# Moving operands at the top of each SBUF partition, weights at the bottom, and four block layouts in the four SwiGLUs

## The chip, the cores and the metric

The kernel runs on one core of one Trainium2 chip. The metric is the time of one execution on the device in microseconds (us). The core has a matrix engine (TensorE, written PE in the profile, with its weight loads listed apart as PEld), a vector engine (DVE), a scalar engine (ACT), a general engine (POOL) and a queue engine (SP). SBUF is the on-chip memory that the engines read. It has 128 partitions, and an address in this text is a byte offset within a partition. PSUM is the memory into which TensorE writes its products.

## What is computed

The reference is a trunk of four residual layers on 256 tokens of 1024 features. Each layer has a token mixer and then a SwiGLU, each behind an RMS norm:

```python
for i in range(DEPTH):                       # DEPTH = 4
    h = rmsnorm(x, norm_mix_g[i])
    # i % 3 == 0: short gated convolution; 1: neighbourhood attention; 2: Hyena long convolution
    x = x + mixer(h)
    x = x + swiglu(rmsnorm(x, norm_ffn_g[i]), f_w13[i], f_w2[i])

def swiglu(h, w13, w2):                      # w13: 1024 x 5632, w2: 2816 x 1024
    g, u = jnp.split(h @ w13, 2, axis=-1)
    return (jax.nn.silu(g) * u) @ w2
```

Layers 0 and 3 use the convolution (mixer A), layer 1 the attention (mixer B), layer 2 the Hyena mixer (mixer C). The Hyena filters depend on the weights alone.

## The kernel before

**Layout.** Features lie on the partitions and the 256 tokens along them, so that every weight is the stationary operand of a matmul (what a weight load, LDWEIGHTS, puts into the array, 128 x 128) and the activations stream past it (the moving operand, 128 x 256).

**Products in three parts.** Every float32 operand is split into a high and a low part of the type float32r. `wload` (line 98) brings a weight piece of 128 x 1024 into a staging tile `st` by a DMA on SP's queue, copies it to `hi` on ACT (line 105) and subtracts to get `lo` on DVE or POOL (the helper on line 74). `mm3` (line 113) then issues three matmuls for each 128 x 128 block: hi by the high part of the moving operand (line 116), hi by its low part (line 117), lo by its high part (line 118). Each has a weight load of its own.

**A SwiGLU** (`ffn`, line 259) first makes 44 column tiles of the gate and up products into the accumulators `pg` and `pu`: 8 blocks, 3 matmuls each, with the normed input `xs` moving (8 tiles `xsf`, each with the high and the low part side by side). That is 1056 matmuls in a layer. `gated` makes the hidden activation and splits it (`split`, line 122) into 11 tiles `hid`. Then come 8 output tiles `po` (line 300) of 22 blocks, taken from weight pieces of 8, 7 and 7 blocks: 528 matmuls with `hid` moving. The mixers use the same helpers, with `xsm` moving in their input products and `mid` tiles in their output products. In mixer B's input product the weights move and `xsm` is the stationary operand.

**Where the tiles lie.** All pools are allocated upwards from one end: constants and `X` first, then `xsp` (`xs`), `wst` (`st`), `wsp` (`hi` and `lo`), the scratch pools, and behind them what a stage needs (`hid`, `mid`, tables). Counting the sizes of the tiles in that order, with the 16 KB and some small constants that the runtime and the compiler keep at the bottom, `xs` begins at 26.0 KB, `hi` at 62.0 KB, `lo` at 86.0 KB. `xs`, `hi` and `lo` tiles are 2 or 4 KB long, so their starts differ by whole multiples of 1 KB. The stage tiles do not keep that: the start of `hid` modulo 1 KB is 672 bytes in layers 0 and 1 and 128 bytes in layers 2 and 3; that of `mid` is 128 bytes in mixers A and C and 800 bytes in mixer B.

**What sets the order.** The source issues everything in the order of use; a scheduler then orders each engine's queue by dependences, among them the reuse of an address by a later tile. The Hyena filters' tables (`filters`, line 542: `dec`, 1 MB, and `dfth`, 512 KB, loaded on ACT's and POOL's queues) share addresses with the `mid` tiles of the first mixer A, and so wait for its output product. The filters' products (`ff`, line 606) are woven into the first two SwiGLUs.

Of the kernel before, what the change touches and what calls it, by code (L numbers as in the profile page):

```python
# [18 lines left out]
P = 128  # L19
# [10 lines left out]
# columns of the per-partition vector table  # L30
# [21 lines left out]
def encoder(ctx: ExitStack, tc: tile.TileContext, A: dict, out: bass.AP):  # L52
    nc = tc.nc
    ve, ac, pe, gp, sy = nc.vector, nc.scalar, nc.tensor, nc.gpsimd, nc.sync

    const = ctx.enter_context(tc.tile_pool(name="const", bufs=1))
    xsp = ctx.enter_context(tc.tile_pool(name="xsp", bufs=8))
    wst = ctx.enter_context(tc.tile_pool(name="wst", bufs=5))
    wsp = ctx.enter_context(tc.tile_pool(name="wsp", bufs=6))
# [16 lines left out]
    def v2(a):  # L76
        """[P, 512] as two halves."""
        return a.rearrange("p (i t) -> p i t", i=2)

# [32 lines left out]

    def mm3(ps, w, ws, xh, xl, first, last, skip=False):
        hi, lo = w
        kw = {"skip_group_check": True} if skip else {}
        pe.matmul(ps, hi[:, ws], xh, start=first, stop=False, **kw)  # L116
        pe.matmul(ps, hi[:, ws], xl, start=False, stop=False, **kw)  # L117
        pe.matmul(ps, lo[:, ws], xh, start=False, stop=last, **kw)  # L118

    def split(hl, src):  # L120
        """hl[:, 0] + hl[:, 1] = src, both float32r; the parts lie along axis 1."""
        ac.copy(out=hl[:, 0], in_=src)
        tt(hl[:, 1], src, hl[:, 0].bitcast(F32), ALU.subtract)

    class Norm:
        """The pre-norm of the next sub-layer: x times the gain as the operand of
        its products, and 1 / rms by token for what comes out of them."""

        def __init__(self, gcol, name):
            self.g, self.name, self.xs, self.late = gcol, name, {}, []  # L130
            self.ss = tp.tile([P, T], F32, tag="ss", name=f"ss{name}", bufs=2)
            self.R, self.some = None, False

        def add(self, m, square=True):
            xm, g = X[:, m, :], vec[:, self.g + m : self.g + m + 1]
            xs = xsp.tile([P, 2, T], F32R, tag="xs", name=f"xs{self.name}_{m}")
            ac.activation(xs[:, 0], xm, AF.Copy, scale=g)
# [20 lines left out]
        def stats(self):  # L158
            """1 / rms, the tokens on the partitions."""
# [13 lines left out]
        def expand(self):  # L173
            """1 / rms along the tokens, on every partition."""
# [14 lines left out]
    def in_tile(ps, w, norm):  # L189
# [4 lines left out]
    def in_group(parts, norm):  # L194
        """Several column tiles side by side, for the first products after a norm:
        (accumulator, weight, whether it is the first of its bank)."""
        for n, (k, xs) in enumerate(norm.xs.items()):
            for ps, w, first in parts:
                mm3(ps, w, slice(k * P, (k + 1) * P), xs[:, 0], xs[:, 1],
                    n == 0 and first, n == KT - 1, skip=True)  # L200

    class OutProj:
        """x += mid @ w, the rows of w as they come."""
# [32 lines left out]
    class Pipeline:  # L236
        """Work in stages, each some slots after the one before it."""
# [12 lines left out]
        def tick(self):  # L250
            """The stages that are due, the oldest work first."""
# [7 lines left out]
    def ffn(layer, norm, nxt, fill):  # L259
        with tc.tile_pool(name=f"ffn{layer}", bufs=NP_) as hp:  # L260
            hid = []

            def gated(j, pg, pu):
# [10 lines left out]
                split(h.rearrange("p i s t -> p s i t"), v2(hh))  # L274
# [4 lines left out]
            for j in range(NP_):  # L279
                pg, pu = bank(f"pg{layer}_{j}"), bank(f"pu{layer}_{j}")  # L280
                parts = []
                for ps, base in ((pg, 0), (pu, FT)):
                    for i in range(2):
# [3 lines left out]
                        if j == 0 and len(parts) == 4:  # L287
                            in_group(parts, norm)
                        elif j:
                            in_tile(*parts[-1][:2], norm)  # L290
# [6 lines left out]
            for m in range(KT):  # L297
# [3 lines left out]
                for k0, k1 in ((0, 8), (8, 15), (15, 22)):  # L301
                    w = wload(A["f_w2"][layer, m][:, k0 * P : k1 * P], (k1 - k0) * P, f"w2_{layer}_{m}_{k0}")
                    for k in range(k0, k1):
                        h = hid[k // 2][:, k % 2]
                        mm3(ps[:, :T], w, slice((k - k0) * P, (k - k0 + 1) * P), h[:, 0], h[:, 1],
                            k == 0, k == FT - 1)
# [24 lines left out]
    def conv3(y, src, wcol, step, m, bcol=None):  # L331
        """Depthwise convolution of width 3 along the tokens."""
# [12 lines left out]
    def mixer_a(ia, norm, nxt, first):  # L345
        with tc.tile_pool(name=f"mixa{ia}", bufs=1) as cp:
# [584 lines left out]
```

## Time and profile before

| what | value |
| --- | --- |
| time, median of 3 runs | 1259.44 us (1259.41 to 1260.6) |
| span of the profiled execution, first to last instruction | 1256.2 us |
| time outside the span (median less span) | 3.2 us |
| mean granted TensorE clock | 0.990 |
| PE busy | 1219.3 us, 97% of the span |
| DVE, ACT, POOL busy | 73%, 51%, 21% |

The own time of the profiled execution is its span. The three runs were timed without a profile. Matmuls are pipelined: one starts before the one before it has ended, so the time that a matmul takes of the engine is the distance between two starts (called spacing here), and not its duration in the trace. The same holds for weight loads, which run beside the matmul before.

### The profile page before, as it was taken

Reading aid. Unit: us, or ns where it says so; the run is one execution under the profiler, and the core shown is the slowest. Engines: PE = TensorE matmul, PEld = TensorE weight load, DVE = VectorE, ACT = ScalarE, POOL = GpSimd, SP = SyncE. Lnnn points to the kernel's source line nnn. Section 1 sums busy time; section 2 is a strip of 40 time slices with the busy share of each in tenths; the row PEclk is TensorE's granted clock in tenths of the full one; section 3 lists DMA queues with packets and bytes.
Section 4 is the critical chain, followed back from the end, with each engine's and each line's share of the span. In section 5 each row is a group of like instructions: output and inputs, shape, how many; then the busy total and the mean of one; then the engine's idle time right before and its main releaser. Section 6 shows DMA issues by size and latency. Waiting matters only on the chain.

```text
span 1256.2 us, 24460 instructions
## 1 busy us (share of the span) xinstructions
PE 1219.3 (97%) x10034; PEld 1211.2 (96%) x10034; DVE 913.4 (73%) x1156; ACT 634.6 (51%) x931; POOL 269.8 (21%) x228
## 2 busy tenths in 40 slices
PE   7999999999999999999988979999999999999998
PEld 7999999999998999999988879999999999999998
DVE  7766877887776688878869997766655676766642
ACT  6545554555667554545544345444444455444431
POOL 0111122333454023213347773000000000000000
PEclk9999999999999999999998989999999999999999
DMA  9556556666666365666754324655566565655571
GB/s 307 184 175 229 185 173 193 201 191 222 209 178 194 118 218 186 192 187 191 232 179 135 121 98 155 199 184 185 173 185 197 176 188 163 199 185 185 170 203 46
DMA packets 68505, 228.90 MB, mean 182 GB/s; under 512 B 9831, under 2 KB 11241, under 8 KB 68265
## 3 DMA queue, kind: packets, MB, share of 16 engines
q1 hardware_dynamic: 61408, 211.68, 53.8%
q0 software_dynamic: 4656, 9.73, 2.6%
q10 hardware_dynamic: 2328, 5.93, 1.4%
q8 instruction: 78, 1.28, 0.4%
q14 instruction: 35, 0.28, 0.1%
HBM read 220.99 MB, written 6.29 MB: 181 GB/s over the span
## 4 chain that ended last, share of the span: by engine, by line
PE 84%; DVE 8%; issue 2%; ACT 2%; DMA 2%; POOL 2%; SPq 0%; ACTq 0%; DVEq 0%; POOLq 0%
PE pu L116 7%; PE pg L116 7%; PE pg L118 7%; PE pu L117 7%; PE pg L117 7%; PE pu L118 7%; PE po L116 7%; PE po L118 7%; PE po L117 7%; DVE a L74 1%; PE ai1a L117 1%; PE ai1a L116 1%; PE ai1a L118 1%; PE accao L116 1%; PE accao L117 1%
## 5 line engine op out<-in xcount | busy, mean ns | idle before, releaser
L105 ACT CAST hiw<-stw 128x1024 fp32r<-128x1024 f32 (+1 forms) x276 | 280.5, 1024 | 314.3 <-PE pg L117 85.3
L74 DVE TENSOR_TENSOR low<-stw,hiw 128x1024 fp32r<-128x1024 f32 (+1 forms) x254 | 306.2, 1212 | 155.1 <-ACT hiw L105 153.8
L116 PE MATMUL pu<-xsf,hiw 128*128 128x256 f32 x704 | 199.9, 284 | 0.0
L116 PE MATMUL pg<-xsf,hiw 128*128 128x256 f32 x704 | 199.3, 283 | 0.0
L118 PE MATMUL pg<-xsf,low 128*128 128x256 f32 x704 | 199.2, 283 | 0.0
L117 PE MATMUL pu<-xsf,hiw 128*128 128x256 f32 x704 | 199.2, 283 | 0.0
L117 PE MATMUL pg<-xsf,hiw 128*128 128x256 f32 x704 | 199.2, 283 | 0.0
L118 PE MATMUL pu<-xsf,low 128*128 128x256 f32 x704 | 199.2, 283 | 0.0
L116 PE MATMUL po<-hid,hiw 128*128 128x256 f32 x704 | 197.5, 281 | 0.0
L117 PE MATMUL po<-hid,hiw 128*128 128x256 f32 x704 | 197.5, 281 | 0.0
L118 PE MATMUL po<-hid,low 128*128 128x256 f32 x704 | 197.5, 281 | 0.0
L116 PEld LDWEIGHTS pg<-xsf,hiw 128*128 128x128 f32 x704 | 134.6, 191 | 0.3 <-issue 0.3
L116 PEld LDWEIGHTS pu<-xsf,hiw 128*128 128x128 f32 x704 | 134.5, 191 | 0.3 <-ACT hiw L105 0.3
L118 PEld LDWEIGHTS pg<-xsf,low 128*128 128x128 f32 x704 | 134.6, 191 | 0.0
L117 PEld LDWEIGHTS pg<-xsf,hiw 128*128 128x128 f32 x704 | 134.6, 191 | 0.0
L117 PEld LDWEIGHTS pu<-xsf,hiw 128*128 128x128 f32 x704 | 134.6, 191 | 0.0
L118 PEld LDWEIGHTS pu<-xsf,low 128*128 128x128 f32 x704 | 134.5, 191 | 0.0
L116 PEld LDWEIGHTS po<-hid,hiw 128*128 128x128 f32 x704 | 132.4, 188 | 0.0
L117 PEld LDWEIGHTS po<-hid,hiw 128*128 128x128 f32 x704 | 132.4, 188 | 0.0
L118 PEld LDWEIGHTS po<-hid,low 128*128 128x128 f32 x704 | 132.4, 188 | 0.0
L74 POOL TENSOR_TENSOR low<-stw,hiw 128x1024 fp32r<-128x1024 f32 (+1 forms) x22 | 53.6, 2434 | 158.8 <-ACT hiw L105 150.8
L105 ACT CAST hiai<-stai 128x1024 fp32r<-128x1024 f32 (+1 forms) x49 | 49.0, 1014 | 49.0 <-issue 13.3
(246 smaller groups left out, 2922.3 us busy)
## 6 DMA issues: line engine op xcount, KB each, us to landing
stw<-in_f_w SPq DMA_DIRECT2D x208, 512.0 KB, 3.6
stw<-in_f_w SPq DMA_DIRECT2D x64, 448.0 KB, 3.4
stai<-in_a_w_in SPq DMA_DIRECT2D x45, 512.0 KB, 3.7
stbi<-in_b_w_qkv SPq DMA_DIRECT2D x24, 512.0 KB, 4.3
stci<-in_c_w_in SPq DMA_DIRECT2D x24, 512.0 KB, 4.0
stao<-in_a_w_out SPq DMA_DIRECT2D x16, 512.0 KB, 4.3
hf<-ht POOLq DMA_DIRECT2D x16, 256.0 KB, 2.7
stbo<-in_b_w_out SPq DMA_DIRECT2D x8, 512.0 KB, 4.0
```

The source lines that it names most:

```text
L74: (eng or ve).tensor_tensor(out=out_, in0=a, in1=b, op=op)
L105: ac.copy(out=hi[:, c], in_=st[:, c])
L116: pe.matmul(ps, hi[:, ws], xh, start=first, stop=False, **kw)
L117: pe.matmul(ps, hi[:, ws], xl, start=False, stop=False, **kw)
L118: pe.matmul(ps, lo[:, ws], xh, start=False, stop=last, **kw)
```

## The change

The pools' order and side change. `wsp` (the weights' parts) now comes first at the bottom, then `wst`, the constants and the scratch; `xsp` and the pools of `hid` and `mid` are allocated from the other end (side="right"). Counted as before, `hi` begins at 16.125 KB, `lo` at 40.125 KB, `hid` lies from 163.97 to 207.97 KB, `mid` from 191.97 to 207.97 KB and `xs` from 207.97 to 223.97 KB. Every moving tile of these kinds now begins 864 bytes, modulo 1 KB, after a weight tile.

Four tables give each layer's SwiGLU a layout. Layer 0 keeps plain blocks. Layer 1 has weight blocks woven element by element: two blocks of w13 side by side (a step of 2 elements when one is loaded), and 8 or 7 blocks of w2 (a step of 8 or 7). Layer 2 has plain weights, and weaves the high and low part of the moving operand in runs of 4 elements. Layer 3 has w13 woven by 8 (a step of 8 elements), and streams the moving operand of w2 backwards, writing PSUM backwards too.

```diff
+GRAIN_13, GRAIN_2 = (0, 2, 0, 8), (0, 8, 0, 0)
+BACK_2 = (False, False, False, True)
+WOVEN_13, WOVEN_2 = (False, False, True, False), (False, False, True, False)
...
+    xsp = ctx.enter_context(tc.tile_pool(name="xsp", bufs=8, side="right"))
+    wsp = ctx.enter_context(tc.tile_pool(name="wsp", bufs=6))
+    wst = ctx.enter_context(tc.tile_pool(name="wst", bufs=5))
     const = ctx.enter_context(tc.tile_pool(name="const", bufs=1))
-    xsp = ctx.enter_context(tc.tile_pool(name="xsp", bufs=8))
-    wst = ctx.enter_context(tc.tile_pool(name="wst", bufs=5))
-    wsp = ctx.enter_context(tc.tile_pool(name="wsp", bufs=6))
...
+    def block(w, ws):
+        if isinstance(ws, slice):
+            return w[:, ws]
+        k, g = ws
+        return w[:, k // g * g * P : (k // g + 1) * g * P].rearrange("p (a g) -> p a g", g=g)[:, :, k % g]
...
-        pe.matmul(ps, hi[:, ws], xh, start=first, stop=False, **kw)
+        pe.matmul(ps, block(hi, ws), xh, start=first, stop=False, **kw)
...
+    def weave(a):
+        return a.rearrange("p s t -> p (s t)").rearrange("p (a s b) -> p s a b", s=2, b=4)
...
+            if self.woven:
+                xs = weave(xs)
...
-            mm3(ps, w, slice(k * P, (k + 1) * P), xs[:, 0], xs[:, 1], n == 0, n == KT - 1)
+            mm3(ps, w, (k, g) if g else slice(k * P, (k + 1) * P), xs[:, 0], xs[:, 1], n == 0, n == KT - 1)
...
-        with tc.tile_pool(name=f"ffn{layer}", bufs=NP_) as hp:
+        with tc.tile_pool(name=f"ffn{layer}", bufs=NP_, side="right") as hp:
...
-                split(h.rearrange("p i s t -> p s i t"), v2(hh))
+                if WOVEN_2[layer]:
+                    for i in range(2):
+                        split(weave(h[:, i]).rearrange("p s a b -> p s a b"),
+                              hh[:, i * T : (i + 1) * T].rearrange("p (a b) -> p a b", b=4))
+                else:
+                    split(h.rearrange("p i s t -> p s i t"), v2(hh))
...
+                        if WOVEN_2[layer]:
+                            h = weave(h)
+                        g = GRAIN_2[layer]
+                        at, po = slice((k - k0) * P, (k - k0 + 1) * P), ps[:, :T]
+                        if BACK_2[layer]:
+                            h, po = h[:, :, ::-1], po[:, ::-1]
+                        mm3(po, w, (k - k0, k1 - k0) if g else at, h[:, 0], h[:, 1], k == 0, k == FT - 1)
...
-            nf = Norm(V_GF + layer * KT, f"f{layer}")
+            nf = Norm(V_GF + layer * KT, f"f{layer}", WOVEN_13[layer])
...
+    w13 = np.stack([woven(a, g) for a, g in zip(_cols(i["f_w13"]), GRAIN_13)])
+    w2 = np.stack([np.concatenate([woven(b, g and b.shape[-1] // P) for b in np.split(a, [8 * P, 15 * P], axis=-1)], axis=-1)
+                   for a, g in zip(_cols(i["f_w2"]), GRAIN_2)])
```

TensorE's and SP's queues keep their order. Two places of other queues do not.

On ACT, in the input product of the first mixer A (`hiai` are the parts of its weights, `sqm` squares for the norm, `Rm` the norm's factors), before:

```order
L155 ACTIVATE sqm_7_312<-X 128x256
L105 CAST hiai_1_264<-stai_1_263 128x1024
L105 CAST hiai_1_324<-stai_1_323 128x1024
L105 CAST hiai_2_375<-stai_2_374 128x1024
L105 CAST hiai_2_420<-stai_2_419 128x1024
L105 CAST hiai_2_450<-stai_2_449 128x1024
L105 CAST hiai_3_482<-stai_3_481 128x1024
L105 CAST hiai_3_527<-stai_3_526 128x1024
```

and with the change:

```order
L178 ACTIVATE sqm_7_312<-X 128x256
L112 CAST hiai_1_264<-stai_1_263 128x1024
L581 CAST onesr<-ones 128x128
L583 DMA zt<-in_zt 33x256
L112 CAST hiai_1_324<-stai_1_323 128x1024
L585 DMA fw_1336<-in_fw 33x128
L587 DMA fw_1338<-in_fw 64x128
L112 CAST hiai_2_375<-stai_2_374 128x1024
L589 DMA fbf<-in_fbf 128x3
L112 CAST hiai_2_420<-stai_2_419 128x1024
L591 DMA dec<-in_dec 128x2048
L112 CAST hiai_2_450<-stai_2_449 128x1024
```

The filters' tables no longer share addresses with `mid`, and their loads on ACT's queue have moved up from behind the mixer's products into its start; on POOL's queue the load of `dfth` has moved to the very first place after the memsets.

On DVE, in the SwiGLU of layer 2 (`hh` is the hidden activation, `hid` its parts, `low` the low part of a weight), before:

```order
L74 TENSOR_TENSOR hh_0_9806<-sg_0_9803,tu_0_9801 128x512
L74 TENSOR_TENSOR tg_1_9873<-pg_1_9696,Rf_9798 128x512
L74 TENSOR_TENSOR low_2_7_10019<-stw_2_7_10017,hiw_2_7_10018 128x1024
L74 TENSOR_TENSOR hid_0_9808<-hh_0_9806,hid_0_9808 128x2x256
L74 TENSOR_TENSOR tu_1_9874<-pu_1_9697,Rf_9798 128x512
```

and with the change:

```order
L81 TENSOR_TENSOR hh_0_9814<-sg_0_9811,tu_0_9809 128x512
L81 TENSOR_TENSOR tg_1_9883<-pg_1_9704,Rf_9806 128x512
L81 TENSOR_TENSOR hid_0_9816<-hh_0_9814,hid_0_9816 128x64x4 x2
L81 TENSOR_TENSOR tu_1_9884<-pu_1_9705,Rf_9806 128x512
L81 TENSOR_TENSOR low_2_7_10033<-stw_2_7_10031,hiw_2_7_10032 128x1024
```

The one subtraction for two halves of `hid` has become two, in runs of 4 elements, and a weight's low part stands behind them instead of ahead.

## Rows read from the trace of the kernel before

**Rows 1.** The page: span and busy time by engine; the granted clock in 40 slices.

```profile
span 1256.2 us, 24460 instructions
...
PE 1219.3 (97%) x10034; PEld 1211.2 (96%) x10034; DVE 913.4 (73%) x1156; ACT 634.6 (51%) x931; POOL 269.8 (21%) x228
...
PEclk9999999999999999999998989999999999999999
```

**Rows 2.** The page: the chain that ended last, shares of the span by engine.

```profile
PE 84%; DVE 8%; issue 2%; ACT 2%; DMA 2%; POOL 2%; SPq 0%; ACTq 0%; DVEq 0%; POOLq 0%
```

**Rows 3.** The page: matmuls and weight loads, count, busy us, mean ns of one.

```profile
L116 PE MATMUL pg<-xsf,hiw 128*128 128x256 f32 x704 | 199.3, 283 | 0.0
...
L116 PE MATMUL po<-hid,hiw 128*128 128x256 f32 x704 | 197.5, 281 | 0.0
```

**Rows 4.** Stretches: their length, PE busy (matmuls touched), granted clock, DMA share, GB/s.

```profile
818.00:898.00 80.00, 80.00 (x669) 1.00 0.58 180
1100.00:1185.00 85.00, 85.00 (x711) 1.00 0.58 180
912.00:968.00 56.00, 56.00 (x474) 1.00 0.65 193
1192.00:1248.00 56.00, 56.00 (x474) 1.00 0.48 139
...
237.40:252.80 15.40, 15.40 (x134) 1.00 0.67 208
253.80:269.20 15.40, 15.40 (x133) 1.00 0.56 163
...
413.00:417.20 4.20, 4.20 (x38) 1.00 0.06 26
```

**Rows 5.** Timeline of PE at one group of filter products: start us, us, instruction.

```profile
165.82 0.28 PE L606 MATMUL ff<-hiw,hd 128*128 128x256 f32 x1
...
166.78 0.28 PE L116 MATMUL pg<-xsf,hiw 128*128 128x256 f32 x1
```

**Rows 6.** Weight loads by tile, ns of one as min/median/max: step 1, step 2, then float32r.

```profile
L441 PEld LDWEIGHTS pqt<-ident,qn x32: 137/141/145, 329.0 to 403.5; 128*128 128x128 f32 x32
...
L678 PEld LDWEIGHTS ut<-ident,cx x8: 196/209/215, 707.0 to 720.6; 128*128 128x128 f32 x8
...
L116 PEld LDWEIGHTS pg<-xsf,hiw x704: 186/192/193, 102.6 to 1183.8; 128*128 128x128 f32 x176
```

**Rows 7.** Timeline of PE: the matmuls behind the loads of step 1 and 2.

```profile
343.69 0.60 PE L441 MATMUL pqt<-ident,qn 128*128 128x128 f32 x4
...
707.07 0.65 PE L678 MATMUL ut<-ident,cx 128*128 128x128 f32 x4
```

**Rows 8.** A stretch of mixer C at half the clock, and PE's timeline in it.

```profile
649.50:652.00 2.50, 2.50 (x14) 2.50 (x14) 1.15 (x3) 1.28 (x4) 1.27 (x2) 0.50 0.77 290
...
650.70 0.41 PE L118 MATMUL uf<-u,dfth 128*128 128x256 f32 x1
650.92 0.41 PE L116 MATMUL uf<-u,dfth 128*128 128x256 f32 x1
```

**Rows 9.** Stretches at the start (busy of PE, PEld, DVE, ACT, POOL), and one wait of ACT.

```profile
15.00:20.00 5.00, 5.00 (x44) 5.00 (x43) 5.00 (x7) 4.03 (x5) 0.00 (x0) 1.00 0.83 249
20.00:25.00 5.00, 5.00 (x44) 5.00 (x43) 3.23 (x5) 2.21 (x3) 0.00 (x0) 1.00 0.95 301
...
22.07 1.05 ACT L105 CAST hiai<-stai 128x1024 fp32r<-128x1024 f32 x1 [2.62 <-DMA stai<-in_a_w_in]
...
120.00:125.00 5.00, 4.62 (x35) 3.91 (x34) 3.23 (x6) 2.37 (x3) 2.18 (x2) 1.00 0.99 338
```

**Rows 10.** Groups of ACT and DVE: the split of 512 elements, and one of 256.

```profile
L122 ACT CAST hid<-hh 128x512 fp32r<-128x512 f32 x44 | 27.3, 620 | 31.0 <-DVE hh L74 31.0
...
L122 ACT CAST midA<-z 128x256 fp32r<-128x256 f32 x16 | 6.5, 407 | 4.1 <-DVE z L74 3.2
...
L74 DVE TENSOR_TENSOR hid<-hh,hid 128x512 fp32r<-128x512 f32 x44 | 36.4, 828 | 5.6 <-ACT hid L122 5.6
...
L74 DVE TENSOR_TENSOR midA<-z,midA 128x256 fp32r<-128x256 f32 x16 | 6.7, 419 | 0.0
```

More of the change, by code (lines that the diff above doesn't have):

```diff
@@ L115, in mm3 @@
         kw = {"skip_group_check": True} if skip else {}
-        pe.matmul(ps, hi[:, ws], xh, start=first, stop=False, **kw)
-        pe.matmul(ps, hi[:, ws], xl, start=False, stop=False, **kw)
-        pe.matmul(ps, lo[:, ws], xh, start=False, stop=last, **kw)
+        pe.matmul(ps, block(hi, ws), xh, start=first, stop=False, **kw)
+        pe.matmul(ps, block(hi, ws), xl, start=False, stop=False, **kw)
+        pe.matmul(ps, block(lo, ws), xh, start=False, stop=last, **kw)
     def split(hl, src):
@@ L123, in split, with __init__ @@
         tt(hl[:, 1], src, hl[:, 0].bitcast(F32), ALU.subtract)
+    def weave(a):
+        return a.rearrange("p s t -> p (s t)").rearrange("p (a s b) -> p s a b", s=2, b=4)
     class Norm:
-        def __init__(self, gcol, name):
+        def __init__(self, gcol, name, woven=False):
             self.g, self.name, self.xs, self.late = gcol, name, {}, []
+            self.woven = woven
             self.ss = tp.tile([P, T], F32, tag="ss", name=f"ss{name}", bufs=2)
@@ L136, in add @@
             xs = xsp.tile([P, 2, T], F32R, tag="xs", name=f"xs{self.name}_{m}")
+            if self.woven:
+                xs = weave(xs)
+            if self.woven:
+                xm = xm.rearrange("p (a b) -> p a b", b=4)
             ac.activation(xs[:, 0], xm, AF.Copy, scale=g)
@@ L187, in residual, with in_tile, in_group @@
             norm.add(m)
-    def in_tile(ps, w, norm):
+    def in_tile(ps, w, norm, g=0):
         for n, (k, xs) in enumerate(norm.xs.items()):
-            mm3(ps, w, slice(k * P, (k + 1) * P), xs[:, 0], xs[:, 1], n == 0, n == KT - 1)
-    def in_group(parts, norm):
+            mm3(ps, w, (k, g) if g else slice(k * P, (k + 1) * P), xs[:, 0], xs[:, 1], n == 0, n == KT - 1)
+    def in_group(parts, norm, g=0):
         for n, (k, xs) in enumerate(norm.xs.items()):
             for ps, w, first in parts:
-                mm3(ps, w, slice(k * P, (k + 1) * P), xs[:, 0], xs[:, 1],
+                mm3(ps, w, (k, g) if g else slice(k * P, (k + 1) * P), xs[:, 0], xs[:, 1],
                     n == 0 and first, n == KT - 1, skip=True)
@@ L287, in ffn @@
                         if j == 0 and len(parts) == 4:
-                            in_group(parts, norm)
+                            in_group(parts, norm, GRAIN_13[layer])
                         elif j:
-                            in_tile(*parts[-1][:2], norm)
+                            in_tile(*parts[-1][:2], norm, GRAIN_13[layer])
                         line.tick()
@@ L345, in mixer_a @@
     def mixer_a(ia, norm, nxt, first):
-        with tc.tile_pool(name=f"mixa{ia}", bufs=1) as cp:
+        with tc.tile_pool(name=f"mixa{ia}", bufs=1, side="right") as cp:
             mids = new_mids(cp, f"A{ia}")
@@ L376, in mixer_b @@
     def mixer_b(norm, nxt):
-        with tc.tile_pool(name="attc", bufs=1) as cp, tc.tile_pool(name="attw", bufs=2) as wp:
+        with (tc.tile_pool(name="attm", bufs=1, side="right") as mp, tc.tile_pool(name="attc", bufs=1) as cp,
+              tc.tile_pool(name="attw", bufs=2) as wp):
             mask = cp.tile([P, 4, P], F32, name="mask")
@@ L387, in mixer_b @@
             part = cp.tile([P, 2, 4], F32, name="part")
-            mids = new_mids(cp, "B")
+            mids = new_mids(mp, "B")
             op = OutProj(A["b_w_out"][0], "bo", AHEAD)
@@ L653, in mixer_c @@
     def mixer_c(norm, nxt):
-        with tc.tile_pool(name="hyc", bufs=1) as cp, tc.tile_pool(name="hyw", bufs=2) as wp:
+        with (tc.tile_pool(name="hym", bufs=1, side="right") as mp, tc.tile_pool(name="hyc", bufs=1) as cp,
+              tc.tile_pool(name="hyw", bufs=2) as wp):
             fc = cp.tile([P, 2, 2, T], F32R, name="dfth")
@@ L658, in mixer_c @@
             gp.dma_start(out=fi, in_=A["dfti"])
-            tiles = [cp.tile([P, 2, 2, T], F32R, name=f"midC{i}") for i in range(4)]
+            tiles = [mp.tile([P, 2, 2, T], F32R, name=f"midC{i}") for i in range(4)]
             mids = [tiles[m // 2][:, m % 2] for m in range(KT)]
@@ L905, in _layout @@
         "c_w_in": _cols(i["c_w_in"]), "c_w_out": i["c_w_out"].reshape(1, KT, P, D),
-        "f_w13": _cols(i["f_w13"]), "f_w2": _cols(i["f_w2"]),
+        "f_w13": w13, "f_w2": w2,
         "rpb": _diagonals(np.pad(i["b_rpb"][0], ((0, 0), (0, 0), (16, 17)))),
```

4 lines of the change are left out of this document (2 added, 2 removed).

## The prediction

> **What bounds the kernel now.** Read first the busy time by engine and the granted clock. [...] The chain that ended last is PE for 84% [rows 2]. So the time is nearly the number of matmuls times their spacing, and whatever lengthens a spacing lengthens the kernel at once, while DVE, ACT and the queues have room.
>
> The durations of the groups, 283 and 281 ns [rows 3], are not spacings, since matmuls overlap. The spacing comes from the stretches: the matmuls touched, divided into the stretch plus one duration. With `xs` moving, 80.28 us / 669 and 85.28 / 711 both give 120.0 ns. With `hid` moving in layers 2 and 3, 56.28 / 474 gives 118.7, twice. With `hid` of layer 0, 15.68 / 134 and 15.68 / 133 give 117.5 in the mean; mixer B's output product gives 4.48 / 38, about 118 [rows 4]. The instructions are the same in form. What differs is where the moving tile starts against the weights: 0, 128, 672 and 800 bytes modulo 1 KB, by the pools' sizes. So addresses matter, by up to 2.5 ns of 120. The steps of the access patterns, the other thing that the change touches, are all 1 in these rows.
>
> **The change part by part.** Sums are made on the profiled execution's span of 1256.2 us and carried to the median by the 3.2 us outside the span.
>
> *Placement.* All moving tiles of `xs`, `hid` and `mid` come to lie 864 bytes after weight tiles, modulo 1 KB, which is 352 modulo 512. The nearest row is the filter products `ff`, where the moving tile starts at the same 352 modulo 512 against its stationary one: 8 of them take 0.96 us, 120 ns each [rows 5]. By that row the 6528 matmuls around `xs` keep their 120.0, and nothing is gained. By the best stretch, 117.5, they would gain 6528 x 2.5 = 16 us, and the 1632 with `hid` of layers 2 and 3 or `mid` of mixers A and C another 2. A loss is bounded by layer 0's `hid` going to 120: 528 x 2.5 = 1 us. I take 0, because the one row with that offset says so, and keep -18 to +1. [...]
>
> *A step in the weights.* Layer 1 loads w13 with a step of 2 (1056 loads) and w2 with a step of 8 or 7 (528), layer 3 loads w13 with a step of 8 (1056). The one strided load in the trace is `ut`, a transposition in mixer C, step 2. It takes 209 ns in the median and 196 at its shortest, where the same load with step 1, `pqt`, takes 141 [rows 6]. So 128 elements with step 2 cost at least 55 ns more than with step 1. Call 55 ns what 128 neighbouring elements cost and 110 what they cost at step 2. The matmuls behind them show it: four take 0.65 us instead of 0.60 [rows 7]; less 0.28 for the last one, (0.65 - 0.28) / 3 = 123 ns against 107.
>
> For step 2 in float32r the bounds are close. A float32r load with step 1 already takes 192 ns [rows 6], as long as the shortest `ut`, behind a spacing of 120, and `ut` with step 2 has 123. I take 0 for layer 1's w13; by 123 it is 1056 x 3 = +3 us, by 117.5 -3.
>
> For steps of 7 and 8 the bounds lie far apart. If only the first doubling costs, the load stays at 110 ns and hides behind the matmul as now: 0. If the cost goes with the stretch read, the load takes 8 x 55 = 440 ns, above any matmul, and the spacing is 440: 1584 x some 320 = +508 us. Between them stands one more doubling, 4 x 55 = 220 ns: two elements that lie 8 bytes apart at step 2 lie 28 or 32 apart at step 7 or 8, so that what is read for one may serve no other. I take 220, nearest to the row in which a doubling of the step doubled the cost and no further than one step from it. The load then sets the spacing: w2 of layer 1 gives 528 x (220 - 117.5) = 54 us, w13 of layer 3 gives 1056 x (220 - 120) = 106 us, together +160. Nothing covers it, since the loads are the very thing that PE waits for, in stretches where PE is never idle [rows 4]. With 209 - 141 = 68 ns instead of 55 it would be 272 and +242 us.
>
> [...]
>
> *Woven moving operand, layer 2.* Runs of 4 elements instead of 256, 1584 matmuls. No row has a moving operand in runs so short. Bounds: 0, and half pace. [...] I take 0: neighbours still come in fours, and at step 2 it was the missing neighbours that cost. On ACT and DVE each split of `hid` becomes two: 2 x 407 - 620 and 2 x 419 - 828 ns [rows 10], at most 0.2 us for each of 11, covered by the idle quarter of DVE and half of ACT. If that cover were gone it would be 2 us.
>
> *Backwards, w2 of layer 3.* 528 matmuls read and write with step -1. [...]
>
> *Loads that move up.* The filters' tables, some 1.6 MB, now load in the first 25 us. There the DMA engines are 0.83 to 0.95 busy and ACT once waits 2.62 us for a weight piece that has not landed [rows 9]. At 300 GB/s 1.6 MB are 5 us. They leave the stretch from 120 to 125 us, where PE lost 0.4 us [rows 9]. I take +2, range 0 to 5. Queued behind the table loads on ACT are only weight casts, which wait for the same DMAs; POOL's early load stands ahead of nothing urgent.
>
> Sum: 1256.2 + 0 + 160 + 2 = 1418 us of span, 1421 us of median.
>
> **The rivals.**
>
> *The steps are hidden (faster, or the same).* A float32r load at step 1 already runs at the pace of a step-2 load, so half of what is read may be wasted today and a step of 8 need not cost more. For it: 192 against 196 ns [rows 6]. Against it: `ut` shows that steps can cost. Then only placement and patterns are left: 1259.4 - 18 - 3 = 1238 at best, 1262 with `ff`'s spacing and the early loads; I would name 1248. It decides at the point where a load of step 8 takes under some 110 ns.
>
> [...]
>
> *Cost by the stretch read, or short runs at half pace.* [...] Against both: they need a unit of reading longer than any row points to.
>
> **How the numbers follow.** Steps cost one doubling and the rest is free: 0.36, 1421 us. Backwards too: 0.15, 1471. Backwards alone: 0.11, 1311. Steps hidden and nothing else costly: 0.28, of which 0.20 faster than by 0.2%, 0.06 within 0.2% (2.5 us, about what can be told from no change) and 0.02 slower. Larger costs: 0.10, 1500 and more. So slower 0.36 + 0.15 + 0.11 + 0.10 + 0.02 = 0.74, same 0.06, faster 0.20. The likeliest is 1421. The range runs from 1240 to 1480: it takes in both rivals around backwards and nearly all of the hidden case, and leaves out the larger costs, the last few us of placement's gain and the end of 272 ns, some 0.16.
>
> **What would show it.** In the trace of the changed kernel, weight loads of `po` in layer 1 and of `pg`, `pu` in layer 3 near 300 ns and their spacing near 220 would show the step's price, against 120 for the rival; in layer 1, `pg` near 120 shows that a step of 2 is free. Layer 0 and the mixers show placement alone: 120.0 if `ff`'s row carries, 117.5 if not. [...] If the loads of layers 1 and 3 stay at 190 ns the prediction is wrong in its main term; if PE waits more before 30 us, the early loads cost more than 2 us.

## The result, and the profile after

The changed kernel takes 1451.99 us in the median (1451.15 to 1453.07), against 1259.43 us for the kernel before in the same session. The ratio is 1.154, with a 95% interval from 1.1523 to 1.1556. It is slower by 192.6 us, where 161.6 were forecast.

The page of the kernel after: its span, busy times, the granted clock in 40 slices, and the groups of `pg` and `po` (mean ns of one behind the busy time).

```profile
span 1449.4 us, 24477 instructions
...
PE 1410.2 (97%) x10034; PEld 1400.5 (97%) x10034; DVE 916.8 (63%) x1167; ACT 635.0 (44%) x942; POOL 268.5 (19%) x228
...
PEclk9999999999999999999999999999999999999999
...
L130 PE MATMUL pg<-xsf,hiw 128*128 128x256 f32 x704 | 220.9, 314 | 0.0
...
L130 PE MATMUL po<-hid,hiw 128*128 128x256 f32 x704 | 219.4, 312 | 0.0
```

Beside [rows 1 to 3]: the number of matmuls is the same, PE is busy for the same 97%, the granted clock is at 0.9 or more of full speed in every slice (0.995 in the mean), and PE has 191 us more of busy time. DVE has 3 us more, ACT 0.4. So PE does not wait for the other engines noticeably more than before: its matmuls have become longer, 314 ns in the mean instead of 283. A mean over four layers hides where; the stretches tell.

Stretches of the kernel after with PE alone (length, busy us and matmuls touched, granted clock, DMA share, GB/s): `w13` of layer 0, `w13` of layer 1 (step 2), `w2` of layer 1 (steps 8 and 7), `w13` and `w2` of layer 2 (woven), `w13` of layer 3 (step 8), `w2` of layer 3 (backwards).

```profile
146.00:164.00 18.00, 18.00 (x152) 1.00 0.56 177
473.00:490.00 17.00, 17.00 (x144) 1.00 0.52 163
596.00:627.00 31.00, 31.00 (x133) 1.00 0.38 110
857.00:967.00 110.00, 110.00 (x928) 1.00 0.61 190
973.00:1034.00 61.00, 61.00 (x515) 1.00 0.63 188
1160.00:1380.00 220.00, 220.00 (x912) 1.00 0.29 89
1385.00:1440.00 55.00, 55.00 (x469) 1.00 0.49 139
```

They are read like [rows 4]: the stretch plus the duration of one matmul, divided by the matmuls touched. That gives 120, 120, 236, 118.8, 119.0, 242 and 117.9 ns. Two of the seven have doubled, and they are the two with a step of 7 or 8 in the weights. Averaged over all starts in the trace, without the breaks between groups, the spacings are 120.0, 120.0, 236.6, 118.9, 118.9, 242.2 and 117.8.

The mechanism is seen in the timeline of both halves of PE in layer 3, `w13` (start us, us, instruction; PEld is the weight load):

```profile
1249.66 0.34 PEld L132 LDWEIGHTS pg<-xsf,low 128*128 128x128 f32 x1
1249.80 0.40 PE L132 MATMUL pg<-xsf,low 128*128 128x256 f32 x1
1249.91 0.34 PEld L130 LDWEIGHTS pg<-xsf,hiw 128*128 128x128 f32 x1
1250.05 0.41 PE L130 MATMUL pg<-xsf,hiw 128*128 128x256 f32 x1
...
1250.15 0.34 PEld L131 LDWEIGHTS pg<-xsf,hiw 128*128 128x128 f32 x1
```

Loads start 0.24 to 0.25 us apart and the matmuls follow at the same distance. Each load's row is 0.34 us long and overlaps the next one, so a row's length is not its price: the price is the distance from start to start.

Step 7 and step 8 do not cost quite the same. In `w2` of layer 1 an output tile takes 24 matmuls at step 8 and then 42 at step 7. The first matmul of a tile, the first at step 7, and the first of the next tile:

```profile
595.56 0.40 PE L130 MATMUL po<-hid,hiw 128*128 128x256 f32 x1
...
601.37 0.41 PE L130 MATMUL po<-hid,hiw 128*128 128x256 f32 x1
...
611.17 0.40 PE L130 MATMUL po<-hid,hiw 128*128 128x256 f32 x1
```

That is 5.81 us / 24 = 242 ns at step 8 and 9.80 us / 42 = 233 ns at step 7; the 236.6 of this product is their mean.

By stage, from the first matmul of one stage to the first of the next, the two executions compare as follows (us; worked out from the starts in the two traces):

| stage | before | after | change |
|---|---|---|---|
| up to layer 0's `w13` (load-up, mixer A) | 102.7 | 104.4 | +1.7 |
| layer 0 `w13` | 134.6 | 134.5 | 0 |
| layer 0 `w2` | 67.2 | 68.5 | +1.3 |
| mixer B | 122.5 | 121.8 | -0.6 |
| layer 1 `w13`, step 2 | 133.3 | 133.4 | 0 |
| layer 1 `w2`, steps 8 and 7 | 66.3 | 129.2 | +63.0 |
| mixer C | 154.2 | 154.3 | +0.1 |
| layer 2 `w13`, woven | 127.1 | 126.0 | -1.2 |
| layer 2 `w2`, woven | 62.7 | 62.8 | +0.1 |
| mixer A of layer 3 | 92.3 | 92.6 | +0.2 |
| layer 3 `w13`, step 8 | 127.1 | 256.2 | +129.1 |
| layer 3 `w2`, backwards, to the end | 66.2 | 65.7 | -0.5 |

The changes add up to 193.2 us, the difference of the two spans. 192.1 of it are the two stepped products. Mixer B's small gain has a place to look for it: in its input product the weights move and `xsm` is stationary, so that its two operands stand otherwise than 352 apart (160 modulo 512, and 0 before), and its 576 matmuls are spaced at 117.2 to 118.9 ns, group by group, where they were at 119.3 to 120.0.

### The profile page after: what moved, and what is told of

The parts are those of the page before. It is cut to its first block, busy times and chain, and to the rows that moved or that the text cites. A ratio compares the mean times of both kernels' runs of the same rounds, so it can differ in the third digit from the quotient of the medians.

```text
span 1449.4 us, 24477 instructions
## 1 busy us (share of the span) xinstructions
PE 1410.2 (97%) x10034; PEld 1400.5 (97%) x10034; DVE 916.8 (63%) x1167; ACT 635.0 (44%) x942; POOL 268.5 (19%) x228
## 4 chain that ended last, share of the span: by engine, by line
PE 88%; DVE 6%; issue 2%; POOL 1%; ACT 1%; DMA 1%; SPq 0%; DVEq 0%; ACTq 0%; POOLq 0%
PE pu L130 7%; PE pg L130 7%; PE po L130 7%; PE pg L132 7%; PE pu L131 7%; PE pu L132 7%; PE pg L131 7%; PE po L132 7%; PE po L131 7%; DVE U L81 1%; PE ai0a L131 1%; PE ai1a L132 1%; PE accao L131 1%; PE accao L132 1%; PE accao L130 1%
## 5 line engine op out<-in xcount | busy, mean ns | idle before, releaser
L130 PE MATMUL pu<-xsf,hiw 128*128 128x256 f32 x704 | 221.4, 315 | 0.0
L130 PE MATMUL pg<-xsf,hiw 128*128 128x256 f32 x704 | 220.9, 314 | 0.0
L131 PE MATMUL pu<-xsf,hiw 128*128 128x256 f32 x704 | 220.1, 313 | 0.0
L131 PE MATMUL pg<-xsf,hiw 128*128 128x256 f32 x704 | 220.1, 313 | 0.0
L130 PE MATMUL po<-hid,hiw 128*128 128x256 f32 x704 | 219.4, 312 | 0.0
L132 PE MATMUL po<-hid,low 128*128 128x256 f32 x704 | 219.2, 311 | 0.0
L131 PE MATMUL po<-hid,hiw 128*128 128x256 f32 x704 | 218.4, 310 | 0.0
L130 PEld LDWEIGHTS pg<-xsf,hiw 128*128 128x128 f32 x704 | 160.8, 228 | 0.3 <-issue 0.3
L130 PEld LDWEIGHTS pu<-xsf,hiw 128*128 128x128 f32 x704 | 160.8, 228 | 0.3 <-ACT Rf L202 0.3
L132 PEld LDWEIGHTS pg<-xsf,low 128*128 128x128 f32 x704 | 160.9, 229 | 0.0
L132 PEld LDWEIGHTS pu<-xsf,low 128*128 128x128 f32 x704 | 160.9, 229 | 0.0
L131 PEld LDWEIGHTS pu<-xsf,hiw 128*128 128x128 f32 x704 | 160.7, 228 | 0.0
L131 PEld LDWEIGHTS pg<-xsf,hiw 128*128 128x128 f32 x704 | 160.7, 228 | 0.0
L130 PEld LDWEIGHTS po<-hid,hiw 128*128 128x128 f32 x704 | 157.9, 224 | 0.0
L132 PEld LDWEIGHTS po<-hid,low 128*128 128x128 f32 x704 | 157.9, 224 | 0.0
L131 PEld LDWEIGHTS po<-hid,hiw 128*128 128x128 f32 x704 | 157.7, 224 | 0.0
```

The lines of the kernel that those rows point to most:

```text
L130: pe.matmul(ps, block(hi, ws), xh, start=first, stop=False, **kw)
L131: pe.matmul(ps, block(hi, ws), xl, start=False, stop=False, **kw)
L132: pe.matmul(ps, block(lo, ws), xh, start=False, stop=last, **kw)
```

## The experiments

Two questions stood after the result. First, what unit the price of a step has: the length that is read over, or the number of pieces of 16 bytes that the operand opens in a partition. Second, whether the place of the tiles does anything by itself, which the spacings between 117.5 and 120 of [rows 4] suggested. In what follows, *difference* means the start of what moves less the start of the weights, in bytes modulo 512; it is 352 for nearly everything in the changed kernel.

### The placement alone

All layouts are plain, the pools stay as the change puts them.

```diff
-GRAIN_13, GRAIN_2 = (0, 2, 0, 8), (0, 8, 0, 0)
-BACK_2 = (False, False, False, True)
-WOVEN_13, WOVEN_2 = (False, False, True, False), (False, False, True, False)
+GRAIN_13, GRAIN_2 = (0, 0, 0, 0), (0, 0, 0, 0)
+BACK_2 = (False, False, False, False)
+WOVEN_13, WOVEN_2 = (False,) * 4, (False,) * 4
```

> The placement of the changed kernel alone: xs, hidden tiles and mids at the top, weights and tables at the bottom, and all eight SwiGLU products read plainly and forwards. Theory (the matmul's spacing goes with where the moving operand starts against the weights, and every plain product of the changed kernel stands at 120.0 ns): the hidden products lose 1.3 to 2.6 ns on each of 4 x 528 matmuls and the mixers' own products about 1.3 on some 900, +4 us, and the early table loads and the half clock at the start +1.5 to 3; together 1263 to 1267 us. Rival (the placement is worth nothing, the whole loss of 192 us lies in the two stepped products): 1258 to 1261. Rival (it parts readers and is a gain): below 1257.

It took 1264.43 us, ratio 1.0042 (1.0026 to 1.0059). So the placement is a small loss, +5.5 us, and the layouts make the other 187. By the same stages as above, the profiled executions differ by 6.3 us: the four `w2` are 4.1 us longer and everything ahead of layer 0's `w13` 2.0 us. Stretches of PE in layer 0's `w2` and in layer 2's `w13`:

```profile
240.00:252.00 12.00, 12.00 (x103) 1.00 0.59 199
785.00:905.00 120.00, 120.00 (x1003) 1.00 0.56 179
```

Both give 119 to 120; the means over all starts are 119.9 and 120.0, where `hid` of layer 0 had 117.5 [rows 4]. The theory held: at the difference 352 everything stands at 120.0.

### The layouts alone

The four layouts as in the change, and every pool where the kernel before has it.

```diff
-    xsp = ctx.enter_context(tc.tile_pool(name="xsp", bufs=8, side="right"))
+    xsp = ctx.enter_context(tc.tile_pool(name="xsp", bufs=8))
...
-        with tc.tile_pool(name=f"ffn{layer}", bufs=NP_, side="right") as hp:
+        with tc.tile_pool(name=f"ffn{layer}", bufs=NP_) as hp:
```

> The four layouts of the changed kernel, and the pools where the kernel before has them (nothing at the top). Theory (the stepped weight loads alone make the loss): layer 1's w2 and layer 3's w13 at 234 to 244 ns as in the changed kernel, and the time below the changed kernel's by what the placement costs, 4 to 7 us: 1444 to 1449 us. Rival (the step's price depends on where the moving operand starts against the weights): spacings off 236.6 and 242.2 by over 5 ns, and a time off 1452 by over 8 us.

It took 1446.19 us in its one execution. Stretches of PE: layer 1's `w2` (steps 8 and 7), layer 2's `w13` (woven), layer 3's `w13` (step 8) and layer 3's `w2` (backwards).

```profile
562.00:592.00 30.00, 30.00 (x128) 1.00 0.34 101
870.00:965.00 95.00, 95.00 (x809) 1.00 0.58 186
1200.00:1370.00 170.00, 170.00 (x706) 1.00 0.28 89
1380.00:1438.00 58.00, 58.00 (x486) 1.00 0.44 132
```

The stepped products are at 236.2 and 241.1 (means over all starts), within 1.1 ns of the changed kernel. The price of a step does not come from the placement, as was expected. The last two products are a hint at something else: woven `xs` has 117.8 here and 118.9 in the changed kernel, and backwards `hid` has 120.0 here and 117.8 there; forwards, at its place here (a difference of 128), it had 118.7 [rows 4].

### Other steps in the weights

```diff
-GRAIN_13 = (0, 2, 0, 8)
+GRAIN_13 = (4, 0, 8, 0)
+# plain: (0, 8, 0), (8, 15, 0), (15, 22, 0), shortened here
+PIECES_2 = (plain, ((0, 6, 3), (6, 12, 3), (12, 18, 3), (18, 22, 0)),
+            plain, ((0, 8, 2), (8, 16, 2), (16, 22, 2)))  # blocks from, to, step
```

> Placement as in plain_top, other steps of the weight's columns: step 4 in layer 0's w13 (1056 matmuls), step 8 in layer 2's w13 (1056), step 3 in 18 of the 22 blocks of layer 1's w2 (432) and step 2 in layer 3's w2 (528). Theory (the price goes by how many pieces of 16 bytes the load opens: step 2 opens 64 of them and is hidden, steps 4 and 8 open 128, one for each element): step 4 is spaced like step 8, 236 to 243 ns, step 3 between 150 and 190, step 2 at 120; 1265 + 2 x 129 + 13 to 30, 1535 to 1555 us. Rival (it goes by the length of the stretch that the load runs over): step 4 stays at or below 135 ns, step 3 at 120, step 8 at 242; 1394 to 1410 us. Rival (any step above 2 costs the same): step 3 at 236 too, near 1574 us.

It took 1535.2 us in its one execution. Stretches of PE: `w13` of layer 0 (step 4, twice), `w2` of layer 1 (step 3), `w13` of layer 2 (step 8), `w2` of layer 3 (step 2).

```profile
231.00:263.00 32.00, 32.00 (x139) 1.00 0.30 97
278.00:310.00 32.00, 32.00 (x137) 1.00 0.30 93
684.00:700.00 16.00, 16.00 (x97) 1.00 0.43 120
1000.00:1170.00 170.00, 170.00 (x704) 1.00 0.28 89
1186.00:1245.00 59.00, 59.00 (x494) 1.00 0.59 186
```

The third stretch holds step 3 and a few plain blocks; step 3 alone is at 175 (median of its starts). So the spacing is 120.0 at step 2, 175 at step 3, 233.3 to 236.7 at step 4 and 242.2 at step 8. Step 4 costs as much as step 7 (233) and within 4% of step 8, though it reads over half the length: the length is not the unit. 128 elements open 64 pieces of 16 bytes at step 2, 96 at step 3 and 128 at step 4 and above. Pieces of 8 bytes would give steps 2, 3 and 4 one price, and pieces of 32 bytes would give step 4 half the price of step 8; neither is seen. Why step 8 has 4% more than steps 4 and 7 is open. 175 / 96 = 1.82 and 233 to 242 / 128 = 1.82 to 1.89 ns for each piece. By the same price step 2 is 64 x 1.82 = 117 ns, which lies just under the 120 of a matmul. That would be why it cost nothing, and it leaves little room. No run has step 2 where plain matmuls are faster than 120.0.

### Other runs of what moves

High and low parts of the moving operand alternate in runs of 2 or 8 or 1 elements, where the change has runs of 4.

```diff
-        return a.rearrange("p s t -> p (s t)").rearrange("p (a s b) -> p s a b", s=2, b=4)
+        return a.rearrange("p s t -> p (s t)").rearrange("p (a s b) -> p s a b", s=2, b=r)
...
+WOVEN_13, WOVEN_2 = (2, 8, 1, 2), (8, 2, 1, 0)  # run of the moving operand
```

> Placement as in plain_top, weights plain; high and low parts of the moving operand alternate in runs of 2 (layer 0's and layer 3's w13, layer 1's w2: 2640 matmuls), of 8 (layer 1's w13, layer 0's w2) and of 1 (layer 2's w13 and w2: 1584 matmuls), where the changed kernel alternates in runs of 4 at 118.9 ns. Theory (a moving read opens 16 bytes at a time, and runs of 4 waste none of them): runs of 8 at 117 to 120, runs of 2 and of 1 at 213 ns or more, near 1265 + 4224 x 0.093 to 0.12 = 1660 to 1770 us. Rival (a moving operand takes one element of 4 bytes for each column and has no such price): all at 117 to 120, 1260 to 1268 us.

It took 1725.81 us in its one execution. Stretches of PE: runs of 2 in layer 0's `w13`, of 8 in layer 1's `w13`, of 2 in layer 1's `w2`, of 1 in layer 2's `w13`.

```profile
231.00:262.00 31.00, 31.00 (x137) 1.00 0.29 98
600.00:625.00 25.00, 25.00 (x213) 1.00 0.67 211
711.00:740.00 29.00, 29.00 (x128) 1.00 0.40 117
1000.00:1190.00 190.00, 190.00 (x832) 1.00 0.30 96
```

Runs of 8 have 118.5 and runs of 4, in the changed kernel, 118.9. Runs of 2 have 228.9 to 235.6, and runs of 1 have 228.9, no more. Pieces of 16 bytes fit again: 256 elements in runs of 4 or 8 open 64 pieces, in runs of 2 or 1 they open 128, and 128 pieces at 1.79 to 1.84 ns are the spacing seen.

Two elements in a piece, with which step 2 of the weights stays at 120.0 ns, are not enough here: runs of 2 have them and go at half pace, 228.9 to 235.6 ns. What fits both experiments is a count of pieces, the larger of the two operands setting the spacing; no run opens 128 pieces in both at once. The plain moving operand opens 64 as well, and its 113.3 to 120.0 ns in the runs below are 1.77 to 1.88 ns for each, so that the plain spacing may be the same price. That is not shown either, since no run moves fewer pieces with as many columns.

### Backwards everywhere

All eight products of the SwiGLU read `xs` or `hid` from the last column to the first and write their accumulator the same way.

```diff
+            if back:
+                xs = xs[:, :, ::-1]
+                ps = ps[:, ::-1]
```

> Placement as in plain_top, and all eight SwiGLU products read what moves, and write their accumulator, from the last column to the first. Theory (reading backwards changes only how the moving stream stands against the weights: where the forward stream is spaced at 120.0 ns the backward one was at 117.8): every SwiGLU matmul at 117.8, 6336 x 2.2 = 14 us under plain_top's 1264.4, 1248 to 1253 us. Rival (the gain in layer 3's w2 belongs to the end of the program or to one product): the others stay at 120.0 and the time at 1260 to 1265. Rival (backwards is dearer in w13, where a PSUM bank has two accumulators): above 1265.

It took 1250.67 us, ratio 0.994 (0.9924 to 0.9957): 13.8 us less than the placement alone, and 0.6% faster than the kernel before. Two groups of layer 0's `w13`, then layer 2's `w13` and `w2`:

```profile
158.00:169.00 11.00, 11.00 (x96) 1.00 0.62 195
176.00:187.00 11.00, 11.00 (x94) 1.00 0.44 148
800.00:899.00 99.00, 99.00 (x843) 1.00 0.58 187
905.00:964.00 59.00, 59.00 (x504) 1.00 0.60 188
```

Nearly all products are at 117.8; in `w13` of layers 0 and 1 one group of eight column tiles each is at 120.0 (second row), which had not been expected. Writing the accumulator downwards, which no run does by itself, shows no price. With the layouts at the bottom backwards was the slower direction (120.0 at a difference of 128, against 118.7 forwards), so that no direction is faster as such. That direction counts only through how the two reads stand to each other fits this and is argued, not shown.

### Other differences

The moving tiles are shifted by up to 480 bytes, in two kernels, so that each product has a difference of its own. Gaps under the hidden tiles come out rounded up to 32 bytes; the differences in the table below are those of the built programs (for `w2` 0, 128, 256 and 384 in place of the 16, 144, 272 and 400 of the expectation).

```diff
-            xs = xsp.tile([P, 2, T], F32R, tag="xs", name=f"xs{self.name}_{m}")
+            at = XS_AT[self.name] // 4
+            xs = xsp.tile([P, 2 * T + XS_SLACK // 4], F32R, tag="xs", name=f"xs{self.name}_{m}")
+            xs = xs[:, at : at + 2 * T].rearrange("p (s t) -> p s t", s=2)
...
+            if HID_LOWER[layer]:
+                padp.tile([P, HID_LOWER[layer] // 4], F32, name=f"fpad{layer}")
```

> Placement as in plain_top, all plain and forwards, but the moving tiles are moved by up to 480 bytes, so that their start less the weights' start, modulo 512, is 32, 64, 96, 192 in the w13 of layers 0 to 3, 224, 256, 320, 384 in their w2, 128 in layer 0's and 160 in layer 3's first mixer product (352, at 120.0 ns, everywhere in plain_top). Theory (the spacing goes with that difference): 116 to 118 at 160 to 288 as the hidden and mid tiles of the kernel before showed, 118 to 120 at 32 to 96, 119 to 120 at 384; 1250 to 1260 us. Rival (it goes with the region or the absolute place): 120.0 everywhere, 1262 to 1266 us.

> As offs_a with other differences: 416, 448, 480, 288 in the w13 of layers 0 to 3, 16, 144, 272, 400 in their w2, 0 and 16 in layer 0's and layer 3's first mixer product. Theory (the spacing goes with the difference): 120.0 at 0, 116.7 to 117.8 at 288 and 272, 117 to 118.7 at 144, 118 to 120 at 400 to 480; 1250 to 1260 us. Rival (region or absolute place): 120.0 everywhere, 1262 to 1266 us.

They took 1247.24 and 1250.01 us, one execution each, the first below its range. From the first kernel, stretches of PE in layer 2's `w13` (difference 96), layer 3's `w13` (192, at its start and later) and layer 2's `w2` (320):

```profile
800.00:900.00 100.00, 100.00 (x836) 1.00 0.56 183
1059.00:1074.00 15.00, 15.00 (x130) 1.00 0.34 105
1100.00:1175.00 75.00, 75.00 (x664) 1.00 0.59 188
906.00:964.00 58.00, 58.00 (x495) 1.00 0.62 192
```

From the second, layer 1's `w13` (448), layer 3's `w13` (288) and layer 2's `w2` (256):

```profile
460.00:490.00 30.00, 30.00 (x265) 1.00 0.57 179
1100.00:1175.00 75.00, 75.00 (x645) 1.00 0.58 184
906.00:964.00 58.00, 58.00 (x486) 1.00 0.62 188
```

Spacings over the starts of each product, forwards and plain. Where two values stand, unbroken stretches of one product differ. Differences that are 256 bytes apart stand in one line:

| difference | spacing, ns | 256 bytes on | spacing, ns |
|---|---|---|---|
| 0 | 120.0 (`xs` before), 119.9 | 256 | 119.9, 120.0 |
| 16 | 118.7 | | |
| 32 | 116.7 and 117.8 | 288 | 116.7 |
| 64 | 113.3 and 117.8 | 320 | 117.8 |
| 96 | 120.0 | 352 | 120.0 (the placement alone) |
| 128 | 118.7 (`hid` before); 118.7 and 120.0 | 384 | 118.7 |
| 160 | 117.4 (`hid` of layer 0 before); 117.4 and 118.7 | 416 | 117.4 and 118.7 |
| 192 | 113.3 and 117.8 | 448 | 113.3 |
| 224 | 118.3 | 480 | 118.3 |

That the spacing goes with the difference held, and that it would be smooth did not: 116 to 118 had been expected over 160 to 288, and there are 113.3 at 192 and 119.9 at 256. Two places, 192 and 448, are better than anything the kernel before has. The lines agree from left to right, so what counts here is the difference modulo 256 bytes. And the difference alone does not fix the spacing: layer 3's `w13` begins with eight column tiles at 117.8 (15.28 us / 130) and goes on at 113.3 (75.28 us / 664), both at 192. In the SwiGLU products of these two kernels a value holds for a whole unbroken stretch, up to 888 matmuls, and changes only where matmuls of something else stand between (filter products, the sums of a norm).

### Are the early table loads the cost at the start?

In the changed kernel the first products are later. PE waits twice for a split of ACT (0.85 and 0.28 us), and then runs at half pace, 0.21 us from start to start, until about 15 us. Timeline of PE in the kernel after, and behind it the same stretch before and after:

```profile
7.83 0.41 PE L132 MATMUL ai0a<-xsm,lofirst 128*128 128x256 f32 x1
9.09 0.58 PE L130 MATMUL ai0a<-xsm,hifirst 128*128 128x256 f32 x1 [0.85 <-ACT xsm L160]
```

```profile
10.50:15.00 4.50, 4.50 (x38) 1.00 1.03 413
10.50:15.00 4.50, 4.12 (x18) 1.00 1.04 407
```

The experiment is the placement alone with layer 0's mixer tiles left at the bottom, so that the tables find no room before that mixer is done:

```diff
-        with tc.tile_pool(name=f"mixa{ia}", bufs=1, side="right") as cp:
+        with tc.tile_pool(name=f"mixa{ia}", bufs=1, side="right" if ia else "left") as cp:
```

> As plain_top, but layer 0's mixer tiles stay at the bottom, over the place that the attention's tables take later, so that those tables are loaded after them as in the kernel before. Theory (the table loads at the start delay the first products, and with them the full clock, by 2 to 3 us): 1261.5 to 1263 us. Rival (the late start has another cause): as plain_top, 1264 to 1265 us.

It took 1263.82 us (1260.74 to 1264.87), ratio 1.004 (1.0027 to 1.0053), which can't be told from the 1264.43 of the placement alone. The tables are loaded after 100 us again, the longer wait of PE is gone, and the half pace stays:

```profile
10.50:15.00 4.50, 4.50 (x21) 1.00 1.02 386
```

21 matmuls in 4.5 us are 214 ns each, close to the 0.22 us at a granted clock of 0.50 in [rows 8], although the row gives the granted clock as 1.00. The output product of the first mixer starts at 81.4 us, as in the changed kernel (81.4), where it started at 79.9 before and at 79.8 with the layouts alone. The placement alone and three more kernels with it and the early loads have 81.7, 80.6, 81.7 and 81.7. So the start is 0.7 to 1.8 us later with the tiles at the top, the early loads are not shown to be a part of it, and its cause is open. Each of these is one execution: before and with the layouts alone the half pace ended at 10.5 and 12.2 us, with the same first matmuls.

### A version that uses the difference

The placement of the change, all products plain, and gaps so that the difference is 448 (192 for the hidden tiles of layers 1 and 2). Beside it the kernel before, with nothing moved to the top, and gaps to the same end.

```diff
+XS_AT = {every norm: 96}            # 448 - 352, bytes; shortened here
+HID_LOWER = (416, 160, 160, 416)
+        pool.tile([P, 416 // 4], F32, name=f"mpad{name}")   # beside the mid tiles
...
+    gap.tile([P, 64 // 4], F32, name="gap")   # in the other kernel, under its weights
```

> plain_top with every moving tile shifted, so that its start less the weights' start, modulo 512 bytes, is 448 (192 for the hidden tiles of layers 1 and 2), the differences that gave 113.33 ns in three of the w13 products so far. Theory (the spacing goes with that difference, whichever product and tile): 113.3 ns in w13 (4224 matmuls), w2 (2112), and the mixers' products (some 2500), 6.67 ns less on each than plain_top: 1264.4 - 28 - 14 - 12 to 17, 1205 to 1212 us. Rival (113.33 is had by xs and w13 alone; the hidden and mid tiles stay near 118): 1225 to 1235 us.

> The kernel before with its pools where they were, and small gaps (64 bytes under the weights, 160 to 320 under hidden and mid tiles), so that every difference is 448 too. Theory (only the difference modulo 512 counts, not which end of the partition a tile lies at): 113.3 ns throughout, and the start of the kernel before kept: 1258.7 - 28 (w13) - 8 to 10 (w2) - 8 (first mixer products) - 4 to 8 (the rest): 1203 to 1211 us, 0 to 5 below top_offset. Rival (what lies at top and bottom matters besides): over 5 us off top_offset.

The first took 1212.47 us, ratio 0.9647 (0.9629 to 0.9664), the second 1227.81 us, ratio 0.9762 (0.9726 to 0.9798). Both beat both kernels. The page of the first, and behind it stretches: two groups of layer 0's `w13`, and layer 2's `w13`.

```profile
span 1210.7 us, 24454 instructions
...
PE 1169.3 (97%) x10034; PEld 1159.5 (96%) x10034; DVE 916.2 (76%) x1156; ACT 632.3 (52%) x931; POOL 271.0 (22%) x228
```

```profile
153.00:164.00 11.00, 11.00 (x96) 1.00 0.57 198
166.00:181.00 15.00, 15.00 (x134) 1.00 0.42 148
800.00:878.00 78.00, 78.00 (x690) 1.00 0.60 189
```

The matmuls are as many as before, and PE is busy for 50 us less. Most groups are at 113.3; the first row, at the same difference as the second, is at 117.8. 1212.47 us is just above the range (1205 to 1212). With the tiles at the bottom more groups are at 117.8, and its executions lie between 1220.4 and 1235.4 us, so it was not what the theory had asked for (1203 to 1211); 15 us above the first, it has the number of the rival by which the ends of the partition matter besides.

Is 448 an edge? The same two kernels with 192 everywhere:

```diff
-XS_AT = {every norm: 96}; HID_LOWER = (416, 160, 160, 416)
+XS_AT = {every norm: 352}; HID_LOWER = (160, 160, 160, 160)
```

> As top_offset with the difference 192 everywhere. Theory (448 is on an edge: some groups of the last two kernels ran at 113.33 and others, at the same difference, at 117.8, while every group seen at 192 ran at 113.33): 113.33 ns in every group, 1207 to 1212 us, 0 to 5 below top_offset. Rival (either value comes at any difference, by the phase in which a group begins): 113.33 and 117.8 side by side, 1212 to 1225 us.

> As bottom_offset (the kernel before with small gaps) with the difference 192 everywhere. Theory (448 is on an edge, 192 is not): 113.33 ns in every group, 1203 to 1211 us, and its runs within 3 us of each other where bottom_offset's lay 15 us apart. Rival (phase at the group's start): spread as in bottom_offset, 1212 to 1230 us.

They took 1213.55 us, ratio 0.9656 (0.9643 to 0.9669), and 1230.13 us, ratio 0.9771 (0.9745 to 0.9797). At the top all SwiGLU products now have 113.3 but for a few tiles, and the time is the same; at the bottom nothing changed. Two neighbouring groups of layer 0's `w13` at the bottom, first with 448, then with 192:

```profile
163.00:179.00 16.00, 16.00 (x138) 1.00 0.46 162
187.00:202.00 15.00, 15.00 (x134) 1.00 0.65 218
...
163.00:179.00 16.00, 16.00 (x138) 1.00 0.48 163
187.00:202.00 15.00, 15.00 (x135) 1.00 0.65 217
```

118 and 113 ns, at one difference, in one product. The theory of an edge at 448 fell, and its premise that every group at 192 had run at 113.33 was not so (layer 3's `w13` above). In the two profiled executions at the bottom, all groups of the SwiGLU products have the same value with 448 as with 192, another sign that 256 bytes more make no difference. What decides between the two values when a stretch begins, and why it falls well more often at the top, is open; that a stretch begins at another phase of the two reads fits the values that hold until the next break, and is not shown.

## Why the prediction was right in sign and short in size

**What bounds the kernel.** That the time is the matmuls' number times their spacing held to the microsecond: 528 x (236.6 - 117.4) = 63 us and 1056 x (242.2 - 120.0) = 129 us are the +63.0 and +129.1 of the stages.

**The steps of 7 and 8, the term that was mis-sized.** It was put at 220 ns of spacing, +160 us; it is 236.6 and 242.2 ns, +192 us. The mechanism that was forecast, that at a step of 7 or 8 a piece that is read for one element serves no other, fits what was measured: the spacing is about double that of step 2 (120.0 ns) from step 4 (233.3 to 236.7) to step 8 (242.2), and does not go with the stretch. The wrong number was the 55 ns for 128 neighbours, taken from the difference of the shortest strided and the median plain load, 196 - 141 [rows 6]; with the median, 68 ns, the working gave 272. The measured value lies between. The experiment with step 3 gives the price that neither row had, 1.82 ns for each piece of 16 bytes, hence 117 for step 2 and 233 and more from step 4 on. That the 7-and-8 product and the 8 product differ by 5.6 ns is the 14 blocks at step 7, at 233 ns beside 242.

**The step of 2: right.** 120.0 in layer 1's `w13`, though a load's row grew from 192 [rows 6] to 198 ns.

**Placement: right where the offset is 352, and its bound too small.** The one row that had the offset, the filter products' 120 ns [rows 5], carried: every plain product at 352 went to or stayed at 120.0. In the changed kernel that is +1.3 us in layer 0's `w2`. The bound of +1 us for a loss counted layer 0's `hid` alone. By the same row the 1632 matmuls at 118.7 go to 120.0 too, 2 us more, and the placement alone shows it with 4.1 us in the four `w2`. The 6528 matmuls "around `xs`" include mixer B's input product, where the weights move: its offset is another, and it gained. What the prediction did not see is that the lever is larger than the 117.5 of its best row: 113.3 ns is to be had.

**Woven and backwards: right, both free.** 118.9 and 117.8 ns, the latter with an accumulator that is written downwards. The bound at half pace was real for shorter runs: 229 ns at runs of 2 and 1. For reading backwards no run shows it, nor the 50 us that 1471 and 1311 are made with: layer 3's `w2`, backwards, took 0.5 us less than before.

**The early loads: the size was right, the cause was not.** +2 us were forecast for them, and the start is 1.5 us later; with the loads back in their place it was no earlier. That the number fits is luck as far as the runs show.

**The rivals.** Steps hidden, with 0.28, falls by the stages of layers 1 and 3. Backwards at half pace, with 0.26, falls by layer 3's `w2` and by the kernel that is backwards throughout. Cost by the stretch falls by step 4; short runs at half pace falls for runs of 4, and holds for 2.

## What to carry to other kernels

Count the pieces of 16 bytes that each operand of a matmul opens: 128 weights of four bytes at a step of 2, or a moving operand in runs of 4, rode along here (120.0 and 118.9 ns), while a step of 4 (233.3 to 236.7 ns) or runs of 2 (228.9 to 235.6) about doubled the spacing, in a kernel that PE bounds. Where PE is busy throughout, work out the spacing from a stretch and its count in every product; if equal products differ by a few per cent, move one tile by 32 to 224 bytes, in steps of 32, before anything else: that brought 2.4% here with gaps alone and 3.5% with the tiles at the top besides, with the same number of matmuls. Before using a strided row as a price, find a second point between it and the case in question.

## What the runs showed of the hardware that was not expected

The distance of the two operands in the partition, modulo 256 bytes, goes with the spacing of 256-column float32r matmuls anywhere from 113.3 to 120.0 ns at the same granted clock (1.00 in the stretches above), and it is no smooth curve (113.3 at 192 and 448, 120.0 at 96, 256 and 352). One distance can have two values, 113.3 and 117.8 or 117.4 and 118.7; a stretch of matmuls keeps its value until others break it. And reading backwards, 117.8 against 120.0 ns forwards at 352, is worth 1% of a kernel there; at 128 it had 120.0 against 118.7, but there forwards too has both values.
